# Memory and first weights in one transfer per row tile, and a closing layer norm without GpSimd

## The chip, the cores and the metric

The kernel runs on one core of a Trainium2 chip. The metric is the device time of one execution in microseconds (us), as the median over several runs. A trace of one profiled execution shows what each engine did: TensorE (PE, with its weight loads as PEld), VectorE (DVE), ScalarE (ACT), GpSimd (POOL) and SyncE (SP), which here only issues transfers.

## The reference

One layer of a hybrid decoder trunk for 256 tokens of width 2,048, in fp32. One input projection feeds eight causal attention heads with rotary positions, a gated MLP and four heads of cross attention into 256 memory tokens; a last projection, the residual and a layer norm close it.

```python
proj = x @ w_in                                   # 2048 x 6656, cut into nine parts
y_mo = moba_attention(rope(q_mo), rope(k_mo), v_mo) * silu(g_mo)   # one block of 256: causal attention
y_gm = gmlp_spatial_gate(u_gm, v_gm, ...) * silu(g_gm)
mem_k, mem_v = split(mem @ w_mem_kv)              # 256 memory tokens
y_me = memory_attention(q_me, mem_k, mem_v) * silu(g_me)
sub = concatenate([y_mo, y_gm, y_me]) @ w_out
x = layer_norm(2 ** 0.25 * x + sub, ln_g, ln_b)   # over the 2048 columns of a token
```

## The kernel before

The precision of fp32 is reached with two parts: an operand is split into a high part in the type float32r and a low part that holds the rest, and a product is made of three matmuls, high by high, high by low and low by high (`mm3`, lines 103 to 107). `split` (lines 99 to 101) makes the high part on ScalarE and then the low part on VectorE.

All weights come in one stream (`STREAM`, lines 39 to 52), in items in the order of use. An item is cut into pieces of 1,024 elements per partition (512 KB). An item marked "T" has 128 columns of weights as the stationary operand and yields the projection transposed (`proj_t`); an item marked "N" has up to 512 columns as the moving operand and yields two PSUM tiles of 128 tokens each (`proj_n`). The 2,048 rows of a contraction are 16 row tiles of 128. `load_piece` (from line 128) takes one of six raw buffers, issues the transfer on SP and splits it into one of four pairs of high and low buffers; `next_pieces` calls it three pieces ahead of use (`LEAD`). Nothing but these buffers, and the order in which the instructions stand on each engine, sets when things happen; a scheduler turns the waits into semaphores.

The first item is the memory's values: `mem` by 512 columns of `w_mem_kv`, 16 row tiles, two PSUM tiles. Both operands must come from memory for it. Its first piece holds two row tiles, and lines 136 to 145 treat them apart. For row tile 0 the memory (128 KB) and the weights (twice 128 KB) come in three transfers and go into exact fp32 matmuls without a split (lines 226 to 231). Row tile 1 comes as 128 KB of memory and 256 KB of weights. From piece 1 on, a transfer of 512 KB of weights and one of 256 KB of memory (`load_act`, line 158) bring two row tiles at a time. Before all that, seven matmuls on zeros (line 114) keep TensorE at work while the first transfers are under way. The items behind it load `x` in the same way, two row tiles at a time.

At the end, the output projection runs over 2,048 columns in items of 512, 512, 512, 256 and 256 (`OUT_COLS`). VectorE adds the residual to each PSUM tile (line 562) and takes the statistics (line 564). In the last item the two token tiles are made one after the other (`apart`), and `finish(t)` (from line 527) closes a token tile: mean and variance, an inverse root on GpSimd (line 334), then five column blocks (`FINISH`). The first block of 512 columns is normed by ScalarE (line 540) and gets gain and bias from GpSimd (lines 541 and 542); the other four (512, 512, 256, 256) are done by VectorE in two steps each, one that subtracts the mean and multiplies by the gain (line 544) and one that multiplies by the inverse root and adds the bias (line 545). SP stores the four blocks of VectorE, the ACT queue that of GpSimd.

## Time and profile before

| | |
|---|---|
| Median of 3 runs | 468.15 us (467.88 to 468.91) |
| Span of the profiled execution | 466.4 us (first to last instruction); its own run time is not given apart from the runs |
| Busy share of the span | PE 96%, PEld 83%, DVE 74%, ACT 50%, POOL 3% |
| Chain that ended last | PE 94%, DVE 3%, DMA 1% |
| Moved by DMA | 91.79 MB, mean 197 GB/s |

The span and all moments are counted from the first instruction. Busy shares are averages over the whole span. In a row of a timeline the first number is the start and the second the duration; what stands in brackets is how long the engine had been idle and what ended it. A duration is longer than the time from one instruction's start to the next one's where an engine overlaps them. The granted clock of TensorE is 1.00 where it runs at its full 2.4 GHz.

### The profile page before, as it was taken

To read this page: it belongs to the slowest core of one execution; us is meant where nothing else is said; L and a number is where in the kernel's file an instruction comes from. 1 tells how busy PE (TensorE), PEld (TensorE's weight loads), DVE (VectorE), ACT (ScalarE), POOL (GpSimd) and SP (SyncE) were. 2 spreads that over 40 slices of the span, in tenths; PEclk is the share of its full clock that TensorE was granted. 3 is DMA by queue.
4 is the path that set the end of the run, shared out by engine and by line. 5 is a ranking of instruction groups with operands and counts; after the bars stand their busy time and mean duration, and the time that the engine had idled before them with its cause. 6 is when DMAs were issued, how large, how long until landed. Compare 5 with 4: busy or idle time off the path is not lost.

```text
span 466.4 us, 6674 instructions
## 1 busy us (share of the span) xinstructions
PE 449.5 (96%) x2465; PEld 386.9 (83%) x2465; DVE 343.5 (74%) x582; ACT 231.3 (50%) x357; POOL 14.4 (3%) x23
## 2 busy tenths in 40 slices
PE   6999999999999999999999999999999999999980
PEld 3888888888888888888888888888888888888980
DVE  3879866776677988885778888858988746465666
ACT  4765754665444555554445545545655543334300
POOL 1000000000000000000000000000200000000033
PEclk9999999999999999999999999999999999999996
DMA  7998776545465555545655455876565557575123
GB/s 268 322 348 275 286 272 225 172 149 161 155 196 179 176 169 182 180 160 163 210 187 180 151 176 200 295 220 204 171 214 181 181 184 237 207 227 184 27 65 135
DMA packets 29552, 91.79 MB, mean 197 GB/s; under 512 B 3408, under 2 KB 5072, under 8 KB 29520
## 3 DMA queue, kind: packets, MB, share of 16 engines
q1 hardware_dynamic: 29232, 90.85, 58.9%
q10 hardware_dynamic: 288, 0.52, 0.3%
q8 instruction: 19, 0.31, 0.3%
q14 instruction: 13, 0.11, 0.1%
HBM read 89.26 MB, written 2.10 MB: 196 GB/s over the span
## 4 chain that ended last, share of the span: by engine, by line
PE 94%; DVE 3%; DMA 1%; SPq 0%; issue 0%; ACT 0%; DVEq 0%
PE acc L195 35%; PE acc L196 18%; PE acc L105 12%; PE acc L106 12%; PE acc L107 12%; DVE hX L544 2%; DMA wraw<-weights 1%; PE ptp L390 1%; DVE hX L545 1%; PE sc L105 1%; PE sc L106 0%; PE sc L107 0%; PE pv L107 0%; PE pv L105 0%; PE pv L106 0%
## 5 line engine op out<-in xcount | busy, mean ns | idle before, releaser
L101 DVE TENSOR_TENSOR wlo<-wraw,whi 128x1024 fp32r<-128x1024 f32 (+1 forms) x152 | 185.5, 1220 | 92.0 <-ACT whi L100 90.7
L100 ACT ACTIVATE whi<-wraw 128x1024 fp32r<-128x1024 f32 (+1 forms) x152 | 160.5, 1056 | 167.6 <-PE acc L195 61.8
L195 PE MATMUL acc<-xX,whi 128*128 128x512 f32 x640 | 227.4, 399 | 0.0
L196 PE MATMUL acc<-xX,wlo 128*128 128x256 f32 x640 | 179.4, 280 | 0.0
L195 PEld LDWEIGHTS acc<-xX,whi 128*128 128x128 f32 x640 | 120.2, 188 | 28.0
L196 PEld LDWEIGHTS acc<-xX,wlo 128*128 128x128 f32 x640 | 120.8, 189 | 0.1
L105 PE MATMUL acc<-whi,yX 128*128 128x512 f32 (+1 forms) x160 | 55.5, 347 | 0.0
L107 PE MATMUL acc<-whi,yX 128*128 128x512 f32 (+1 forms) x160 | 55.5, 347 | 0.0
L106 PE MATMUL acc<-wlo,yX 128*128 128x512 f32 (+1 forms) x160 | 55.5, 347 | 0.0
L105 PE MATMUL acc<-whi,xX 128*128 128x512 f32 x96 | 38.1, 397 | 0.0
L107 PE MATMUL acc<-whi,xX 128*128 128x512 f32 x96 | 37.5, 391 | 0.0
L106 PE MATMUL acc<-wlo,xX 128*128 128x512 f32 x96 | 37.4, 390 | 0.0
L105 PEld LDWEIGHTS acc<-whi,yX 128*128 128x128 f32 x160 | 30.3, 189 | 3.8
L107 PEld LDWEIGHTS acc<-whi,yX 128*128 128x128 f32 x160 | 30.3, 189 | 3.8
L106 PEld LDWEIGHTS acc<-wlo,yX 128*128 128x128 f32 x160 | 30.3, 189 | 3.7
L195 PE MATMUL acc<-memX,whi 128*128 128x512 f32 x64 | 22.6, 399 | 0.0
L107 PEld LDWEIGHTS acc<-whi,xX 128*128 128x128 f32 x96 | 18.0, 188 | 4.0
L105 PEld LDWEIGHTS acc<-whi,xX 128*128 128x128 f32 x96 | 18.0, 188 | 3.4
L106 PEld LDWEIGHTS acc<-wlo,xX 128*128 128x128 f32 x96 | 18.0, 188 | 3.3
L202 DVE TENSOR_TENSOR projT<-acc,part 128x256 f32<-128x256 f32 x44 | 18.1, 413 | 0.0
L196 PE MATMUL acc<-memX,wlo 128*128 128x256 f32 x64 | 18.0, 281 | 0.0
L200 ACT ACTIVATE part<-acc 128x256 f32<-128x256 f32 x44 | 16.1, 369 | 0.0
(147 smaller groups left out, 411.0 us busy)
## 6 DMA issues: line engine op xcount, KB each, us to landing
wraw<-weights SPq DMA_DIRECT2D x151, 512.0 KB, 3.5
araw<-xT SPq DMA_DIRECT2D x8, 256.0 KB, 4.5
araw<-memT SPq DMA_DIRECT2D x7, 256.0 KB, 5.8
xs<-xrow SPq DMA_DIRECT2D x6, 256.0 KB, 4.4
lnp<-ln_gv SPq DMA_DIRECT2D x4, 256.0 KB, 4.5
lnp<-ln_bv SPq DMA_DIRECT2D x4, 256.0 KB, 5.3
out<-hX SPq DMA_DIRECT2D x4, 256.0 KB, 2.6
xs<-xrow SPq DMA_DIRECT2D x4, 128.0 KB, 3.3
```

What stands on the lines that cost most here:

```text
L100: nc.scalar.activation(hi, src, AF.Copy)
L101: nc.vector.tensor_tensor(out=lo, in0=src, in1=f32(hi), op=ALU.subtract)
L105: nc.tensor.matmul(o, a[0], b[0], start=start, stop=False)
L106: nc.tensor.matmul(o, a[0], b[1], start=False, stop=False)
L107: nc.tensor.matmul(o, a[1], b[0], start=False, stop=stop)
L195: nc.tensor.matmul(flat, hi[:, m, :], X[:, k].rearrange("p a s -> p (a s)"), start=k == 0, stop=False)
L196: nc.tensor.matmul(acc[:, 0, :], lo[:, m, :], X[:, k, 0, :], start=False, stop=k == KT - 1)
L200: nc.scalar.activation(part, acc[:, 1, :], AF.Copy)
L202: nc.vector.tensor_tensor(out=r, in0=acc[:, 0, :], in1=part, op=ALU.add)
L390: nc.tensor.transpose(tp[:, n, :], st["p"][:, at[t] // P + b, :], ident)
L544: nc.vector.scalar_tensor_tensor(out=o, in0=o, scalar=mvr[:, 0:1], in1=g, op0=ALU.subtract, op1=ALU.mult)
L545: nc.vector.scalar_tensor_tensor(out=o, in0=o, scalar=rs, in1=b, op0=ALU.mult, op1=ALU.add)
```

## The change

The first item becomes an item of its own kind, "H". The host lays each row tile of the memory (256 columns) beside the 512 columns of weights of the same rows, 768 elements per partition, 384 KB without a gap, and one transfer brings both (line 142 of the new kernel). There are 16 such pieces of one row tile each, where 8 pieces of two row tiles and as many transfers of memory were before. All 16 row tiles are split and take six matmuls each; the four exact matmuls of row tile 0 go. In row tile 0 VectorE makes the memory's high part, in the others ScalarE. The pieces use the same six raw buffers and the four pairs of split buffers. In this item the matmuls of both PSUM tiles alternate, first high by high, then memory low by weights high, then memory high by weights low. `mm3` takes the same order everywhere.

In `finish` VectorE does all five blocks in its two steps. Two subtract steps (`AHEAD`) stand ahead of the first step that needs the inverse root. ScalarE's pass, GpSimd's two passes and the product of mean and inverse root go. The stores go in turn through the ACT queue (blocks 0, 2 and 4) and the SP queue (blocks 1 and 3).

```diff
+STREAM = [("H", "mem", 4 * P, NW)] + [("T", "mem", b) for b in range(4)]
-STREAM = [("N", "mem", 4 * P, NW)] + [("T", "mem", b) for b in range(4)]
...
+AHEAD = 2
...
 def pieces_of(item):
+    if item[0] == "H":
+        return KT, 1, item[3]
...
     def mm3(o, a, b, start, stop):
         nc.tensor.matmul(o, a[0], b[0], start=start, stop=False)
-        nc.tensor.matmul(o, a[0], b[1], start=False, stop=False)
-        nc.tensor.matmul(o, a[1], b[0], start=False, stop=stop)
+        nc.tensor.matmul(o, a[1], b[0], start=False, stop=False)
+        nc.tensor.matmul(o, a[0], b[1], start=False, stop=stop)
...
     def load_piece(n):
...
-        if n == 0:
-            a = wp.tile([P, S], F32, tag="araw", name="araw0", bufs=3)
-            nc.sync.dma_start(a, memT[:, 0, :])
-            for c in range(0, width, S):
-                nc.sync.dma_start(raw[:, 0, c:c + S], src[:, 0, c:c + S])
-            first.update(a=a, w=raw[:, 0, :])
-            load_act(memT, memX, 1, 1)
-            nc.sync.dma_start(raw[:, 1, :], src[:, 1, :])
-            split(hi[:, 1, :], lo[:, 1, :], raw[:, 1, :])
+        if STREAM[i][0] == "H":
+            both = wp.tile([P, PIECE], F32, tag="wraw", name="hraw", bufs=6)[:, :S + width]
+            nc.sync.dma_start(both, head[j])
+            if j == 0:
+                nc.vector.tensor_copy(memX[:, j, 0, :], both[:, :S])
+            else:
+                nc.scalar.activation(memX[:, j, 0, :], both[:, :S], AF.Copy)
+            nc.vector.tensor_tensor(out=memX[:, j, 1, :], in0=both[:, :S], in1=f32(memX[:, j, 0, :]), op=ALU.subtract)
+            split(hi[:, 0, :], lo[:, 0, :], both[:, S:])
         else:
-            nc.sync.dma_start(raw, src)
+            raw = wp.tile([P, kts, width], F32, tag="wraw", name="wraw", bufs=6)
+            nc.sync.dma_start(raw, w[n - KT].rearrange("p (k n) -> p k n", k=kts))
             split(hi, lo, raw)
-        if n == 1:
-            split(memX[:, 0, 0, :], memX[:, 0, 1, :], first["a"])
-        if 0 < n < first_piece[1]:
-            load_act(memT, memX, kts * n, kts)
...
     def proj_n(X, order=range(KT), hook=None, apart=False):
...
-                if X is memX and k == 0:
-                    for c in range(0, width, S):
-                        for t in range(NT):
-                            nc.tensor.matmul(acc[t][:, c:c + S], first["a"][:, t * P:(t + 1) * P],
-                                             first["w"][:, c:c + S], start=c == 0, stop=False)
-                    continue
+                if X is memX:
+                    for a, b in ((0, hi), (1, hi), (0, lo)):
+                        for t in range(NT):
+                            nc.tensor.matmul(acc[t], X[:, k, a, tk[t]], b[:, m, :], start=k == 0 and a == 0 and b is hi,
+                                             stop=k == KT - 1 and b is lo)
...
     def finish(t):
...
-        nm = work.tile([P, 1], F32, tag="nm", name="nm")
-        neg = work.tile([P, 1], F32, tag="neg", name="neg")
-        nc.vector.tensor_scalar(out=neg, in0=mvr[:, 0:1], scalar1=-1.0, scalar2=None, op0=ALU.mult)
-        nc.gpsimd.tensor_tensor(out=nm, in0=neg, in1=rs, op=ALU.mult)
-        for c, wd in FINISH:
-            cs, ls = slice(c, c + wd), slice(c % NW, c % NW + wd)
-            o, g, b = hX[:, t, cs], lg[c // NW][:, ls], lb[c // NW][:, ls]
-            if c == 0:
-                nc.scalar.activation(o, o, AF.Identity, scale=rs, bias=nm)
-                nc.gpsimd.tensor_tensor(out=o, in0=o, in1=g, op=ALU.mult)
-                nc.gpsimd.tensor_tensor(out=o, in0=o, in1=b, op=ALU.add)
-            else:
-                nc.vector.scalar_tensor_tensor(out=o, in0=o, scalar=mvr[:, 0:1], in1=g, op0=ALU.subtract, op1=ALU.mult)
-                nc.vector.scalar_tensor_tensor(out=o, in0=o, scalar=rs, in1=b, op0=ALU.mult, op1=ALU.add)
-            if c:
-                nc.sync.dma_start(out[t, :, cs], o)
-        cs = slice(0, FINISH[0][1])
-        nc.scalar.dma_start(out[t, :, cs], hX[:, t, cs])
+        def centre(c, wd):
+            o, g, _ = part(c, wd)
+            nc.vector.scalar_tensor_tensor(out=o, in0=o, scalar=mvr[:, 0:1], in1=g, op0=ALU.subtract, op1=ALU.mult)
+
+        for c, wd in FINISH[:AHEAD]:
+            centre(c, wd)
+        for n, (c, wd) in enumerate(FINISH):
+            if n >= AHEAD:
+                centre(c, wd)
+            o, _, b = part(c, wd)
+            nc.vector.scalar_tensor_tensor(out=o, in0=o, scalar=rs, in1=b, op0=ALU.mult, op1=ALU.add)
+            (nc.sync if n % 2 else nc.scalar).dma_start(out[t, :, c:c + wd], o)
...
+    memT, c = stationary(mem), STREAM[0][2]
+    head = np.concatenate([memT.transpose(1, 0, 2), mats["mem"][:, c:c + NW].reshape(KT, P, NW)], axis=2)
```

The order of the transfers on SP at the start, before:

```order
L138 DMA araw_108<-memT 128x256
L140 DMA wraw<-weights 128x256 x2
L160 DMA araw<-memT 128x256
L143 DMA wraw<-weights 128x512
L146 DMA wraw<-weights 128x1024
L160 DMA araw<-memT 128x512
L146 DMA wraw<-weights 128x1024
L160 DMA araw<-memT 128x512
L146 DMA wraw<-weights 128x1024
```

and now:

```order
L142 DMA hraw<-head 128x768 x16
L151 DMA wraw<-weights 128x1024 x4
L161 DMA araw<-xT 128x512
L261 DMA posi<-pos 128x256
L263 DMA invf<-inv_freq 128x1
L151 DMA wraw<-weights 128x1024
L161 DMA araw<-xT 128x512
```

Ten issues of 128 to 512 KB, for the first six row tiles and the weights of two more, have become one issue per row tile (`hraw` is a raw buffer with both operands, `head` the tensor in memory).

TensorE's first matmuls on data, before (`araw_108` is the memory's row tile 0):

```order
L229 MATMUL acc<-wraw,araw_108 128x256 x4
L105 MATMUL acc<-whi,memX 128x512 x2
L106 MATMUL acc<-wlo,memX 128x512
L107 MATMUL acc<-whi,memX 128x512
L106 MATMUL acc<-wlo,memX 128x512
L107 MATMUL acc<-whi,memX 128x512
L105 MATMUL acc<-whi,memX 128x512 x2
L106 MATMUL acc<-wlo,memX 128x512 x2
```

and now, from row tile 0 on:

```order
L231 MATMUL acc<-whi,memX 128x512 x4
L231 MATMUL acc<-wlo,memX 128x512 x2
L231 MATMUL acc<-whi,memX 128x512 x4
L231 MATMUL acc<-wlo,memX 128x512 x2
L231 MATMUL acc<-whi,memX 128x512 x4
L231 MATMUL acc<-wlo,memX 128x512 x2
```

The unsplit fp32 product is gone, and every row tile reads four times with the high weights before it needs the low ones.

VectorE from the inverse root's input of the first token tile to the second tile's residual step (`omv` mean and variance, `ors` the inverse root, `lnp` gain or bias), before:

```order
L333 TENSOR_SCALAR rsq<-omv 128x1
L534 TENSOR_SCALAR neg<-omv 128x1
L544 SCALAR_TENSOR_TENSOR hX<-hX,omv,lnp 128x512 x2
L545 SCALAR_TENSOR_TENSOR hX<-hX,ors,lnp 128x512 x2
L544 SCALAR_TENSOR_TENSOR hX<-hX,omv,lnp 128x256 x2
L545 SCALAR_TENSOR_TENSOR hX<-hX,ors,lnp 128x256 x2
L562 SCALAR_TENSOR_TENSOR hX<-xs,acc 128x256
L564 BN_STATS obn_3790<-hX 128x6
```

and now:

```order
L334 TENSOR_SCALAR rsq<-omv 128x1
L539 SCALAR_TENSOR_TENSOR hX<-hX,omv,lnp 128x512 x2
L547 SCALAR_TENSOR_TENSOR hX<-hX,ors,lnp 128x512 x2
L539 SCALAR_TENSOR_TENSOR hX<-hX,omv,lnp 128x512
L539 SCALAR_TENSOR_TENSOR hX<-hX,omv,lnp 128x256
L547 SCALAR_TENSOR_TENSOR hX<-hX,ors,lnp 128x512
L547 SCALAR_TENSOR_TENSOR hX<-hX,ors,lnp 128x256
L539 SCALAR_TENSOR_TENSOR hX<-hX,omv,lnp 128x256
L561 SCALAR_TENSOR_TENSOR hX<-xs,acc 128x256
L547 SCALAR_TENSOR_TENSOR hX<-hX,ors,lnp 128x256
L563 BN_STATS obn_3834<-hX 128x6
```

Two steps of 512 columns have come in, the negation has gone, and the residual step of the second tile stands ahead of the last scale step of the first.

## Rows read from the trace of the kernel before

**Rows 1.** Page: the head

```profile
span 466.4 us, 6674 instructions
```

**Rows 2.** Busy time by stretch: PE, PEld, DVE, ACT, POOL; clock, DMA share, GB/s

```profile
4.00:12.20 8.20, 5.71 (x21) 3.35 (x21) 3.04 (x5) 3.81 (x6) 0.00 (x0) 1.00 0.93 347
12.20:453.00 440.80, 440.80 (x2439) 382.35 (x2438) 329.98 (x558) 224.98 (x349) 7.55 (x10) 1.00 0.60 197
```

**Rows 3.** PE waits, 0 to 12.5 us: us in total, times, longest

```profile
PE acc L105 <- ACT whi L100: 1.5, 1, 1.5
PE acc L105 <- ACT memX L100: 1.0, 1, 1.0
```

**Rows 4.** ACT timeline, first stage: start us, us; what ended its wait

```profile
3.04 0.42 ACT L100 ACTIVATE memX<-araw 128x256 fp32r<-128x256 f32 x1 [0.96 <-DMA araw<-memT]
4.95 0.42 ACT L100 ACTIVATE memX<-araw 128x256 fp32r<-128x256 f32 x1 [1.49 <-DMA araw<-memT]
6.89 0.63 ACT L100 ACTIVATE whi<-wraw 128x512 fp32r<-128x512 f32 x1 [1.53 <-DMA wraw<-weights]
8.86 1.06 ACT L100 ACTIVATE whi<-wraw 128x1024 fp32r<-128x1024 f32 x1 [1.33 <-DMA wraw<-weights]
24.24 0.63 ACT L100 ACTIVATE memX<-araw 128x512 fp32r<-128x512 f32 x1 [1.51 <-DMA araw<-memT]
```

**Rows 5.** PE timeline, either end of the unbroken first item

```profile
12.40 0.40 PE L105 MATMUL acc<-whi,memX 128*128 128x512 f32 x1
30.09 0.39 PE L195 MATMUL acc<-memX,whi 128*128 128x512 f32 x1
```

**Rows 6.** DVE timeline of the first closing norm

```profile
448.88 0.14 DVE L534 TENSOR_SCALAR neg<-omv 128x1 f32<-128x1 f32 x1
448.94 0.74 DVE L544 SCALAR_TENSOR_TENSOR hX<-hX,omv,lnp 128x512 f32<-128x512 f32 x1
451.59 1.51 DVE L544 SCALAR_TENSOR_TENSOR hX<-hX,omv,lnp 128x256 f32<-128x256 f32 x1
453.03 1.48 DVE L544 SCALAR_TENSOR_TENSOR hX<-hX,omv,lnp 128x256 f32<-128x256 f32 x1
454.44 0.87 DVE L545 SCALAR_TENSOR_TENSOR hX<-hX,ors,lnp 128x256 f32<-128x256 f32 x2
```

**Rows 7.** POOL timeline beside it

```profile
449.12 0.98 POOL L334 TENSOR_TENSOR ors<-rsq 128x1 f32<-128x1 f32 x1 [119.38 <-DVE neg L534]
451.32 1.50 POOL L541 TENSOR_TENSOR hX<-hX,lnp 128x512 f32<-128x512 f32 x1 [0.93 <-ACT hX L540]
452.90 1.33 POOL L542 TENSOR_TENSOR hX<-hX,lnp 128x512 f32<-128x512 f32 x1
```

**Rows 8.** SP timeline: the last store

```profile
462.97 0.41 SPq L547 DMA_DIRECT2D out<-hX  x1
```

**Rows 9.** SP timeline at the start (moments of issue)

```profile
0.80 0.39 SPq L138 DMA_DIRECT2D araw<-memT  x1
2.66 0.43 SPq L143 DMA_DIRECT2D wraw<-weights  x1
```

**Rows 10.** Tile wraw, 250 to 330 us: issue to landing of 512 KB

```profile
DMA to landing us min/median/max: 3.1/3.4/5.1
```

**Rows 11.** ACT by form, 0 to 36 us: count, busy us, mean ns, idle

```profile
L100 ACT ACTIVATE memX<-araw 128x256 fp32r<-128x256 f32 x2 | 0.8, 416 | 2.4 <-DMA araw<-memT 2.4
L100 ACT ACTIVATE whi<-wraw 128x512 fp32r<-128x512 f32 x1 | 0.6, 629 | 1.5 <-DMA wraw<-weights 1.5
```

**Rows 12.** DVE by form, 0 to 36 us, same columns

```profile
L101 DVE TENSOR_TENSOR memX<-araw,memX 128x256 fp32r<-128x256 f32 x2 | 0.8, 425 | 3.8 <-ACT memX L100 3.8
L101 DVE TENSOR_TENSOR wlo<-wraw,whi 128x512 fp32r<-128x512 f32 x1 | 0.7, 693 | 1.7 <-ACT whi L100 1.7
```

**Rows 13.** DVE timeline, low parts of the next three weight pieces

```profile
26.72 3.78 DVE L101 TENSOR_TENSOR wlo<-wraw,whi 128x1024 fp32r<-128x1024 f32 x3 [1.12 <-ACT whi L100]
```

**Rows 14.** DMA issues, 448 to 467 us: count, KB each, us to landing

```profile
out<-hX ACTq DMA_DIRECT2D x2, 256.0 KB, 2.6
```

More of the change, by code (lines that the diff above doesn't have):

```diff
@@ L76, in hymba_layer @@
 @with_exitstack
-def hymba_layer(ctx: ExitStack, tc: tile.TileContext, xT, memT, x, pos, inv_freq, w, wsT, b_s,
+def hymba_layer(ctx: ExitStack, tc: tile.TileContext, xT, head, x, pos, inv_freq, w, wsT, b_s,
                 gln_g, gln_b, ln_g, ln_b, out):
@@ L125, in hymba_layer @@
             first_piece[i] = n
-    ready, first = {}, {}
+    ready = {}
     def load_piece(n):
@@ L205, in proj_n @@
     def proj_n(X, order=range(KT), hook=None, apart=False):
-        assert STREAM[item[0]][0] == "N"
+        assert STREAM[item[0]][0] in "HN"
         width = STREAM[item[0]][3]
@@ L225, in proj_n @@
                 k = order[j * kts + m]
-                if X is memX and k == 0:
-                    for c in range(0, width, S):
+                tk = [slice(t * P, (t + 1) * P) for t in range(NT)]
+                if X is memX:
+                    for a, b in ((0, hi), (1, hi), (0, lo)):
                         for t in range(NT):
-                            nc.tensor.matmul(acc[t][:, c:c + S], first["a"][:, t * P:(t + 1) * P],
-                                             first["w"][:, c:c + S], start=c == 0, stop=False)
-                    continue
-                for t in range(NT):
-                    tk = slice(t * P, (t + 1) * P)
-                    mm3(acc[t], (X[:, k, 0, tk], X[:, k, 1, tk]), (hi[:, m, :], lo[:, m, :]),
-                        j + m == 0, j * kts + m == KT - 1)
+                            nc.tensor.matmul(acc[t], X[:, k, a, tk[t]], b[:, m, :], start=k == 0 and a == 0 and b is hi,
+                                             stop=k == KT - 1 and b is lo)
+                else:
+                    for t in range(NT):
+                        mm3(acc[t], (X[:, k, 0, tk[t]], X[:, k, 1, tk[t]]), (hi[:, m, :], lo[:, m, :]),
+                            j + m == 0, j * kts + m == KT - 1)
                 pump()
@@ L531, in finish, with part @@
         rsqrt(rs, mvr[:, 1:2], LN_EPS)
[L532 to L549 removed]
+        def part(c, wd):
+            return hX[:, t, c:c + wd], lg[c // NW][:, c % NW:c % NW + wd], lb[c // NW][:, c % NW:c % NW + wd]
+        def centre(c, wd):
[9 more added lines that the diff above has]
+            (nc.sync if n % 2 else nc.scalar).dma_start(out[t, :, c:c + wd], o)
     for n, (c, wd) in enumerate(OUT_COLS):
@@ L578 @@
     stream = []
-    for item in STREAM:
+    memT, c = stationary(mem), STREAM[0][2]
+    head = np.concatenate([memT.transpose(1, 0, 2), mats["mem"][:, c:c + NW].reshape(KT, P, NW)], axis=2)
+    for item in STREAM[1:]:
         n, kts, width = pieces_of(item)
@@ L585 @@
         "xT": stationary(x),
-        "memT": stationary(mem),
+        "head": head,
         "xrow": x[0].reshape(NT, P, D),
```

2 lines of the change are left out of this document (removed).

## Prediction

> **What bounds the kernel now.** I read the page's head, then the busy time by stretch, the waits of TensorE, the timelines of the first stage, and last the timelines of VectorE, GpSimd and the stores at the end. The profiled span is 466.4 us [rows 1]. The runs give no separate time for the profiled execution; their median, 468.15 us, is 1.75 us above the span, and I carry these 1.75 us over.
>
> The reader should see three parts. From 12.20 to 453.00 us TensorE is busy for 440.80 of 440.80 us, with the granted clock at 1.00 [rows 2]: nothing ends a wait there, and only fewer matmuls could shorten it. Before that, from 4.00 to 12.20 us, it is busy for 5.71 of 8.20 us [rows 2]. Both of its waits for data lie there: 1.5 us for the high part of the first weights and 1.0 us for that of the memory, both made by ScalarE [rows 3]. ScalarE in turn waits for transfers [rows 4]. In that stage ScalarE starts as each transfer lands, so its starts give the arrivals: 128 KB by 3.04 us, 512 KB by 4.95, 768 KB by 6.89, 1,280 KB by 8.86, and all 6,144 KB of the first item (memory and weights) by 24.24 us [rows 4]. The third part is the time after the last matmul, some 13 us, where VectorE works off two closing norms and the last store goes out at 462.97 us [rows 8].
>
> The first item's last matmul is followed by the next item at 30.09 us [rows 5]. Between 12.40 and 30.09 us lie 13 row tiles of 6 matmuls, so one takes 17.69/78 = 0.227 us and a row tile 1.36 us. The question at the start is how much earlier than 30.09 us the next item begins; since TensorE never pauses after that, all of it reaches the end.
>
> **The start.** The change removes the four exact fp32 matmuls of row tile 0 and gives it six split ones like the others: 96 matmuls, 96 x 0.227 = 21.8 us. If they ran without a pause from moment t, the next item would begin at t + 21.8.
>
> *When can they start?* One transfer of 384 KB is issued at the same 0.80 us [rows 9]. 128 KB landed 2.24 us after that issue [rows 4, 9], and 512 KB take at least 3.1 us [rows 10]; 384 KB two thirds of the way between are 2.8 us, landing at 3.6. ScalarE then makes the high weights in 0.63 us [rows 11] and TensorE starts some 0.05 us later, at 4.3. The seven warming matmuls, unchanged, stand ahead of it; I allow 0.1 us for them. VectorE makes the memory's high and low parts in under 0.9 us, and the low weights in 0.69 us [rows 12], which the order high-high, low-high, high-low covers: the first four matmuls take 0.9 us. So t = 4.4 and the best case is 4.4 + 21.8 = 26.2 us, a gain of 3.9.
>
> *Does piece 1 come in time?* Its ScalarE work is 0.42 + 0.63 us [rows 11], so it can be used 1.1 us after landing, and 15 row tiles (20.4 us) follow. In the kernel before, 768 KB had landed at 6.89 us [rows 4], with the last of them issued at 2.66 us [rows 9]. Now two issues make up these 768 KB; at the old pitch of four issues in 1.86 us [rows 9] the second goes at 1.27, 1.4 us sooner. I take the landing 1.4 us sooner too, at 5.5 us: use at 6.6, next item at 6.6 + 20.4 = 27.0 us. The worst case keeps the old arrivals by bytes: piece 1 at 6.89, piece 2 (1,152 KB, between the last two arrivals) at 8.4; 8.4 + 1.1 + 14 x 1.36 = 28.5 us. The gain thus lies between 1.6 and 3.9 us; I take **3.0**, from the shifted arrival, whose row is nearest in bytes.
>
> *Later pieces.* From 8.86 to 24.24 us 4,864 KB came [rows 4], 1.21 us for 384 KB, less than the 1.36 us in which TensorE uses them. Per piece ScalarE has 1.05 us of work and VectorE 1.12 [rows 11, 12]; both fit. The six raw buffers let six transfers queue, so SP waits on VectorE's last read of a buffer only from piece 6 on. Even unchanged arrivals would do for the last piece: 24.24 + 1.1 + 1.36 = 26.7 us. Of the next item's weights, the first low part was ready at 26.72 + 1.26 = 28.0 us before [rows 13]; were it no earlier, TensorE would pause under 0.8 us there. I count nothing, as no transfer of the stage gets later and the pieces behind it have 2 us and more in hand.
>
> Here a rule speaks against the change. The row says that 256 and 512 KB transfers, queued behind one another, came at 4,864 KB in 15.4 us [rows 4], so their fixed time overlaps. The Trainium skill, page "DMA: Bandwidth & Descriptors", section "Bandwidth", would have transfers batched to at least 1 MiB, and this change cuts some from 512 to 384 KB. By the row the term stays 3.0; by that rule it would shrink or turn, which is the third rival.
>
> **The order of the three products** (high-low last, everywhere) moves no time: TensorE waits for nothing after 12.20 us [rows 2], and the number of loads and matmuls per row tile is the same.
>
> **The end.** VectorE's two passes over 512 columns cost 2.65 us for four steps from 448.94 to 451.59, 0.66 each; the two 256-column subtract steps take 1.44 and 1.41 us from start to start, though half as wide, and the two 256-column scale steps 0.87 together [rows 6]. The slow ones stand exactly beside GpSimd's two passes over 512 columns: these end at 452.82 and 454.23, VectorE's at 453.10 and 454.51, each 0.28 us later [rows 6, 7]. I read this as VectorE held until GpSimd is done. The change takes those passes and ScalarE's away and gives VectorE two more 512-column steps. Per row block: before 2.65 + 2.85 + 0.87 = 6.37; now 6 x 0.66 + 4 x 0.435 = 5.7. That saves 0.66, and the dropped negation 0.06 [rows 6]. Both blocks lie end to end on VectorE (the second accumulator is complete soon after 453.00 us [rows 2], VectorE is free only at 454.44 + 0.87 = 455.31 [rows 6]), so twice 0.72 = 1.44. The last scale step now follows directly on its own input, and starts when that ends: under 0.1 us back. **1.4**.
>
> Is the inverse root late? GpSimd gives it at 449.12 + 0.98 = 450.10 us [rows 7]; two subtract steps from 448.88 end their turn at 450.20. The margin is 0.1 us, so at worst some tenths come back: 1.2 at the low end, 1.5 at the high. The store queues: SP's old issues wait on VectorE, not on each other; ACT's stores land in 2.6 us [rows 14], and each waits only for VectorE. ScalarE has nothing else to do then. Splitting the stores over two queues counts nothing, and the last store moves with VectorE's end.
>
> **Sum.** 466.4 - 3.0 - 1.4 = 462.0 us of span, + 1.75 = **463.7 us**.
>
> **The rivals.** *Early transfers stay as slow as now* (0.15): the arrivals by bytes do not move, the start gains 1.6 and the end 1.2 to 1.4, 465.2 us. For it: from 4.95 to 6.89 us only 256 KB landed, with five transfers already issued. Against: the old stage began with four transfers of 128 KB, issue by issue.
>
> *The narrow subtract step is slow of itself* (0.04): then each block costs 3.96 + 2.85 + 0.87 = 7.7 us, 1.3 more than now, less the negation; the end loses 2.5, and 466.4 - 3.0 + 2.5 + 1.75 = 467.6, no change that can be told. Against it: 512 columns take half that time.
>
> *The smaller pieces come more slowly than TensorE uses them* (0.03), the side on which it is slower. The slowest stretch of the trace brought 768 KB from 4.95 to 8.86 us [rows 4], 1.95 us for 384 KB. At that pace the last piece lands at 3.6 + 15 x 1.95 = 32.9, the next item starts 2.5 us later at 35.4 against 30.09, and with the end's 1.4 the kernel takes 468.15 + 5.3 - 1.4 = 472 us. It turns slower from 1.7 us per piece on: (30.09 + 1.4 - 2.5 - 3.6)/15. This is where the skill's rule on batching would bite; the rows after 8.86 us speak against it.
>
> *The start gains but the next item waits for its weights* (0.05): up to 0.8 us back, 464.5.
>
> **How the numbers follow.** The forecast has the remaining 0.73; with its bounds (start 2.2 to 3.9, end 1.2 to 1.5) it reaches from 462.7 to 464.8. Adding the first and the last rival, and a little for run to run, the range is 462.4 to 465.6. A measurement tells about 0.2%, 0.94 us, from no change. Faster: 0.73 + 0.15 + 0.05 = 0.93; same: 0.04; slower: 0.03.
>
> **What would show it.** Right: the second item's first matmul near 27 us, TensorE's only wait between row tiles 0 and 1, at most about 1 us; no pause after that; subtract steps of 256 columns near 0.45 us; the last store 4 to 5 us earlier. Wrong: TensorE waiting for ScalarE at every row tile (pace), a 256-column step still near 1.4 us (not GpSimd), or VectorE idle before the first scale step (inverse root late).

## The result, and the profile after

The changed kernel takes 463.77 us (median of four runs, 463.63 to 464.22); the kernel before, on the same chip, 468.15 us (467.88 to 468.91). The ratio is 0.9897, 95% interval 0.9878 to 0.9917. The profiled execution took 463.88 us with a span of 462.2 us, 1.68 us more than the span.

Busy time by stretch answers to [rows 2]; columns as there, the last stretch ends with the last store's issue:

```profile
4.00:12.20 8.20, 7.55 (x29) 5.28 (x29) 6.37 (x14) 5.89 (x13) 0.00 (x0) 1.00 0.97 348
12.20:448.00 435.80, 435.80 (x2407) 377.80 (x2406) 326.10 (x563) 223.83 (x356) 4.13 (x7) 1.00 0.57 198
448.00:459.00 11.00, 2.84 (x24) 2.63 (x22) 10.83 (x22) 0.00 (x0) 0.93 (x1) 0.83 0.46 160
```

TensorE is now busy for 7.55 of the first 8.20 us instead of 5.71, and still without a gap in the long middle. Its waits for data in the first 30 us (us in total, times, longest) answer to [rows 3]:

```profile
PE acc L231 <- ACT whi L106: 0.6, 2, 0.3
```

So 2.5 us of waiting became 0.6, but still in two places. ScalarE's timeline gives the arrivals, as in [rows 4]: the first start, and each start after a wait for a transfer, is a row tile that has landed.

```profile
3.80 0.63 ACT L106 ACTIVATE whi<-hraw 128x512 fp32r<-128x512 f32 x1 [1.73 <-DMA hraw<-head]
5.47 0.42 ACT L146 ACTIVATE memX<-hraw 128x256 fp32r<-128x256 f32 x1 [1.04 <-DMA hraw<-head]
...
7.47 0.42 ACT L146 ACTIVATE memX<-hraw 128x256 fp32r<-128x256 f32 x1 [1.06 <-DMA hraw<-head]
...
8.55 0.42 ACT L146 ACTIVATE memX<-hraw 128x256 fp32r<-128x256 f32 x1
```

Row tiles 0, 1 and 2 are there at 3.80, 5.47 and 7.47 us; from row tile 3 on ScalarE finds each one waiting. TensorE's timeline shows what that costs:

```profile
4.49 1.27 PE L231 MATMUL acc<-whi,memX 128*128 128x512 f32 x4
...
6.46 1.19 PE L231 MATMUL acc<-whi,memX 128*128 128x512 f32 x4 [0.24 <-ACT whi L106]
...
8.46 1.20 PE L231 MATMUL acc<-whi,memX 128*128 128x512 f32 x4 [0.34 <-ACT whi L106]
...
9.95 1.07 PE L231 MATMUL acc<-whi,memX 128*128 128x512 f32 x4
...
27.63 0.39 PE L196 MATMUL acc<-memX,whi 128*128 128x512 f32 x1
```

From start to start, waits included, row tiles 0 and 1 take 1.97 and 2.00 us each, row tile 2 1.49, all others 1.36. The next item starts at 27.63 us instead of 30.09 [rows 5]: 2.46 us. In the kernel before, TensorE came to row tile 2 here:

```profile
10.48 0.73 PE L105 MATMUL acc<-whi,memX 128*128 128x512 f32 x2 [0.98 <-ACT memX L100]
```

So it is there 10.48 - 8.46 = 2.02 us sooner: 1.39 us because the row tile lands at 7.47 us instead of 8.86 [rows 4], and 0.63 us because ScalarE's work takes 0.99 us from there to TensorE's start instead of 1.62, as a transfer brings one row tile and not two. Nearly all of the other 0.44 us lie in row tile 2 itself, which took 1.92 us before (to 12.40 [rows 5]) and now takes 1.49.

The end, VectorE's timeline of the second closing norm (the first one's steps have the same durations), beside [rows 6]:

```profile
445.12 0.42 DVE L561 SCALAR_TENSOR_TENSOR hX<-xs,acc 128x256 f32<-128x256 f32 x1 [3.55 <-PE acc L113]
...
453.17 1.40 DVE L539 SCALAR_TENSOR_TENSOR hX<-hX,omv,lnp 128x512 f32<-128x512 f32 x2
454.50 1.41 DVE L547 SCALAR_TENSOR_TENSOR hX<-hX,ors,lnp 128x512 f32<-128x512 f32 x2
455.82 1.14 DVE L539 SCALAR_TENSOR_TENSOR hX<-hX,omv,lnp 128x512 f32<-128x512 f32 x2
456.88 1.14 DVE L547 SCALAR_TENSOR_TENSOR hX<-hX,ors,lnp 128x512 f32<-128x512 f32 x2
457.94 0.48 DVE L539 SCALAR_TENSOR_TENSOR hX<-hX,omv,lnp 128x256 f32<-128x256 f32 x1
458.45 0.48 DVE L547 SCALAR_TENSOR_TENSOR hX<-hX,ors,lnp 128x256 f32<-128x256 f32 x1
```

(A pair of 1.14 us is one step of 512 columns and one of 256; the view gives the first one's form.) The 256-column subtract step takes 0.48 us instead of 1.48 to 1.51, and nothing waits for the inverse root, which is GpSimd's only work left [rows 7]:

```profile
446.67 0.92 POOL L335 TENSOR_TENSOR ors<-rsq 128x1 f32<-128x1 f32 x1 [119.33 <-DVE rsq L334]
453.40 0.93 POOL L335 TENSOR_TENSOR ors<-rsq 128x1 f32<-128x1 f32 x1 [5.81 <-DVE rsq L334]
```

In the kernel before, the first closing residual stood here:

```profile
447.57 0.42 DVE L562 SCALAR_TENSOR_TENSOR hX<-xs,acc 128x256 f32<-128x256 f32 x1 [3.44 <-PE acc L107]
```

The last store, ScalarE's queue (the issue) and the issues from 458.5 us on (count, KB, us to landing), beside [rows 8, 14]:

```profile
458.97 0.34 ACTq L548 DMA_DIRECT2D out<-hX  x1
```

```profile
out<-hX ACTq DMA_DIRECT2D x1, 128.0 KB, 2.1
```

From the first closing residual of the last columns to the last store's issue it was 462.97 - 447.57 = 15.40 us; it is 458.97 - 445.12 = 13.85, 1.55 us less. From there to the span's end 3.43 us became 3.23. So 2.46 + 1.55 + 0.20 = 4.2 us, which is the whole difference of the spans; from the second item's first matmul to the first closing residual both kernels take 417.48 us to within 0.01.

### The profile page after: what moved, and what is told of

The parts are those of the page before. It is cut to its first block, busy times and chain, and to the rows that moved or that the text cites. A ratio compares the mean times of both kernels' runs of the same rounds, so it can differ in the third digit from the quotient of the medians.

```text
span 462.2 us, 6713 instructions
## 1 busy us (share of the span) xinstructions
PE 448.9 (97%) x2463; PEld 386.6 (84%) x2463; DVE 343.8 (74%) x600; ACT 231.2 (50%) x369; POOL 6.6 (1%) x17
## 4 chain that ended last, share of the span: by engine, by line
PE 94%; DVE 3%; DMA 1%; issue 0%; ACT 0%; SPq 0%
PE acc L196 36%; PE acc L197 18%; PE acc L111 11%; PE acc L113 11%; PE acc L112 11%; PE acc L231 4%; DMA hraw<-head 1%; DVE hX L547 1%; PE ptp L391 1%; DVE hX L539 1%; PE sc L111 1%; PE sc L112 0%; PE sc L113 0%; PE pv L113 0%; PE pv L111 0%
## 5 line engine op out<-in xcount | busy, mean ns | idle before, releaser
L107 DVE TENSOR_TENSOR wlo<-wraw,whi 128x1024 fp32r<-128x1024 f32 x144 | 176.1, 1224 | 86.9 <-ACT whi L106 84.8
L106 ACT ACTIVATE whi<-wraw 128x1024 fp32r<-128x1024 f32 x144 | 152.3, 1059 | 159.2 <-PE acc L196 58.0
L231 PE MATMUL acc<-whi,memX 128*128 128x512 f32 x64 | 17.6, 396 | 0.6 <-ACT whi L106 0.6
```

The source lines that it names most:

```text
L106: nc.scalar.activation(hi, src, AF.Copy)
L107: nc.vector.tensor_tensor(out=lo, in0=src, in1=f32(hi), op=ALU.subtract)
L231: nc.tensor.matmul(acc[t], X[:, k, a, tk[t]], b[:, m, :], start=k == 0 and a == 0 and b is hi, stop=k == KT - 1 and b is lo)
```

## Experiments

Each was run beside the kernel before on the same chip; ratios are to that kernel.

### The start alone, the end alone

The closing norm of the kernel before, put into the changed kernel, and the reverse:

```diff
 # e1: finish(t) is that of the kernel before; all else as in the changed kernel
 # e2: the kernel before, with finish(t) of the changed kernel and
+AHEAD = 2
```

> The change's start and its order of the three products, with the closing norm of the kernel before (ScalarE and GpSimd take the first block, negation included). Theory: start and end add up and do not touch each other; the second item begins at about 27.6 us as after the change, the last store goes out some 15.4 us after the first closing residual step as before, total 468.15 - 2.5 = 465.7 us (465.3 to 466.0). Rival: what the start gains is worth less or more once the end is the old one (the store tail or the weights at the end hold it); then the total is under 465 or over 466.5 us.

> The kernel before with the change's closing norm alone. Theory: GpSimd's passes held VectorE; without them the closing work from the first residual step to the last store takes 13.85 us instead of 15.4, total 468.15 - 1.6 = 466.5 us (466.2 to 466.9); 256-column subtract steps at 0.48 us. Rival: the narrow subtract step is slow of itself; then they stay near 1.4 us and the total is 470 us or more.

The start alone: 465.55 us (465.03 to 466.0), ratio 0.9927 [0.9901, 0.9953]; its second item starts at 28.01 us, and its 256-column subtract steps are slow as before, 2.92 and 2.88 us for two. The end alone: 467.69 us (465.84 to 468.24), ratio 0.9967 [0.9947, 0.9987]; 256-column steps of 0.48 us, and again 13.85 us from the first closing residual to the last store's issue. By the ratios, 0.73% and 0.33% come to 1.06%, beside the whole change's 1.03%, but each of them is known to 0.2 or 0.3% only, and six of the twelve runs of the kernel before that they are measured against lie in the upper group that the last experiment is about. The traces are firmer. From the second item to the first closing residual it is 417.48 us in both, as before and as after the change; from there to the last store's issue it is 15.4 us with the old end and 13.85 with the new. The two parts add up and do not touch each other. That the end alone came 1.2 us above the expectation has another cause, which follows below.

### What sets the start

Four edits, each undoing or moving one thing: the old order of the products in `mm3`, that is everywhere but in the first item, which keeps its own new order; row tile 0 unsplit; memory and weights of a row tile in two transfers on the same queue; and ScalarE's copy of the memory put on VectorE.

```diff
 # e3, mm3
-        nc.tensor.matmul(o, a[1], b[0], start=False, stop=False)
-        nc.tensor.matmul(o, a[0], b[1], start=False, stop=stop)
+        nc.tensor.matmul(o, a[0], b[1], start=False, stop=False)
+        nc.tensor.matmul(o, a[1], b[0], start=False, stop=stop)
 # e9, load_piece
-            nc.sync.dma_start(both, head[j])
+            nc.sync.dma_start(both[:, :S], head[j][:, :S])
+            nc.sync.dma_start(both[:, S:], head[j][:, S:])
 # e4, load_piece; VectorE keeps the order copy, memory low, weights low
-            if j == 0:
+            if j < 3:
                 nc.vector.tensor_copy(memX[:, j, 0, :], both[:, :S])
 # e8, proj_n: row tile 0 is multiplied as it is, memory is split beside row tile 3
+                if X is memX and k == 0:
+                    for c in range(0, width, S):
+                        for t in range(NT):
+                            nc.tensor.matmul(acc[t][:, c:c + S], first["a"][:, t * P:(t + 1) * P],
+                                             first["w"][:, c:c + S], start=c == 0, stop=False)
```

> The changed kernel with the old order of the three products outside the first item (high-high, high-low, low-high). Theory: TensorE waits for no operand after the first stage, so the order is worth nothing: 463.8 us, within 0.3. Rival: the low weights come late somewhere in the output projection or the attention and the new order hides it; then TensorE shows waits after 12 us and the total rises by 0.5 us or more.

> The changed kernel with each piece of the first item brought by two transfers, 128 KB of memory and 256 KB of weights, instead of one of 384 KB; everything else as changed. Theory: what one transfer per row tile buys at the start is issue time; two issues of some 0.46 us per piece put the second piece's last issue at 2.2 us instead of 1.25, and its arrival 0.5 to 1 us later than 5.5 us: second item at 28.1 to 28.6 us, total 464.3 to 464.8 us. Rival: the arrivals are set by the transfer engines alone, not by the issues; then the second piece still lands at 5.5 us and the total stays at 463.8 us.

> The changed kernel, with the high part of memory's row tiles 1 and 2 made on VectorE and no longer on ScalarE, so that ScalarE makes only the weights' high part there (0.6 us after a transfer lands, and no copy of memory ahead of it). In the changed kernel TensorE waits 0.24 us before row tile 1 and 0.34 us before row tile 2 for ScalarE's copies. My theory (part of the lost start is the two copies in series on ScalarE behind each arrival): the weights' high part of row tiles 1 and 2 is ready about 0.25 us earlier, the second item starts at 27.2 to 27.5 us instead of 27.63, and the time falls by 0.2 to 0.4 us to 463.3 to 463.6 us. Rival (TensorE waits for the transfers alone, and VectorE's copy, its low part behind it, makes the weights' low part later by as much): second item at 27.6 to 27.8, time 463.7 to 464.0 us.

> The changed kernel with row tile 0 as an unsplit fp32 product again (eight matmuls of 256 columns, 1.89 us in the profile of before, in place of six of 512 columns behind the copy), loaded by the new single transfer; memory's two parts of row tile 0 are made later, beside row tile 3. My theory (TensorE waits for row tiles 1 and 2 in any case, so a row tile 0 that starts 0.6 us earlier and takes 0.5 us longer moves nothing): second item at 27.4 to 27.9 us, time 463.5 to 464.2 us, the same as the changed kernel. Rival (splitting row tile 0 was part of the gain): second item at 28.1 us or later, time 464.3 to 465.0 us.

Measured: e3 463.87 us, ratio 0.9893 [0.9871, 0.9915]; e9 463.97, 0.9904 [0.9876, 0.9933]; e4 463.51, 0.9896 [0.9880, 0.9913]; e8 463.78, 0.9896 [0.9877, 0.9915]. None can be told from the changed kernel. For e9 that is a miss of mine in the time, but not in the arrivals:

```profile
4.41 0.63 ACT L106 ACTIVATE whi<-hraw 128x512 fp32r<-128x512 f32 x1 [2.33 <-DMA hraw<-head]
...
6.56 0.63 ACT L106 ACTIVATE whi<-hraw 128x512 fp32r<-128x512 f32 x1 [1.21 <-DMA hraw<-head]
```

```profile
7.24 1.21 PE L232 MATMUL acc<-whi,memX 128*128 128x512 f32 x4 [0.48 <-ACT whi L106]
```

With two issues for each row tile, row tiles 0 and 1 are complete 0.6 and 1.1 us later than in the changed kernel (3.80 and 5.47 us), as I had expected. But the memory of row tile 1 lands ahead of its weights and is copied by then, TensorE can use the row tile 0.68 us after it has landed, and it does not wait for row tile 2: its last wait is the one before row tile 1, and the second item starts at 27.81 us, 0.18 us later than in the changed kernel. So bringing both operands in one transfer makes the first row tiles earlier and still buys no time that the runs can tell.

In the others the last wait is for row tile 2. Where it lands, and where the second item starts, in us from the span's start:

| kernel | row tile 2 landed | second item | between |
|---|---|---|---|
| changed | 7.47 | 27.63 | 20.16 |
| e1, old end | 7.85 | 28.01 | 20.16 |
| e3, old product order | 7.49 | 27.65 | 20.16 |
| e6, one store queue (below) | 7.57 | 27.73 | 20.16 |
| e8, row tile 0 unsplit | 7.33 | 27.50 | 20.17 |
| e4, memory's copy on VectorE | 7.64 | 27.50 | 19.86 |

Whatever is done to row tiles 0 and 1 here, the item starts a fixed time after row tile 2's landing: ScalarE's two copies and 14 row tiles. Only e4 changes that, by 0.30 us, since there the memory's copy is off ScalarE; it lands in the time as 0.1 to 0.3 us, less than the runs tell apart (e6, run beside it with the changed kernel's start, took 463.54 us). Splitting row tile 0 is worth nothing by itself. So of what the change does to the start, neither the split nor the single transfer explains the 2.46 us when taken alone. What is left is the size of a piece, one row tile instead of two, and the order of the products within the first item; no run changes one of these alone, so it stays an argument that the size does it.

### Why row tile 2 lands late

Between 4 and 6 us the transfer engines move 200 and 264 GB/s, half to two thirds of what they do later. That is not all. For each transfer the trace keeps 16 marks of completion, as many as the core has transfer engines, and the transfer has landed with the last of them. In the changed kernel row tile 0's marks lie between 3.35 and 3.78 us. Of row tile 1's, fifteen are there by 4.76 us and the last comes at 5.45. Of row tile 2's, eight are there by 6.12 us and fifteen by 6.66, and the last comes at 7.45, when nine of row tile 3's are there already. The other five kernels of the table show the same: half of row tile 2 by 5.69 to 6.15 us, the last mark at 7.31 to 7.83. So what TensorE waits for is the last parts of row tile 2, while parts of later row tiles are already complete. Three edits bring in the second queue; all three also keep SyncE's other loads in their place, and e13 the first steps of VectorE and ScalarE.

```diff
 # e7: six raw buffers are filled at once, in turn by two queues
+                (nc.scalar if e in (1, 3, 5) else nc.sync).dma_start(early[e], head[e])
 # e10: each of the six in two halves of 64 partitions
+                    nc.sync.dma_start(early[e][:P // 2], head[e][:P // 2])
+                    nc.scalar.dma_start(early[e][P // 2:], head[e][P // 2:])
 # e13: e4, and ScalarE issues row tiles 2 and 4 behind a tiny activation
+                nc.scalar.activation(tiny[:, 1:2], tiny[:, 0:1], AF.Copy)
+                (nc.scalar if e in (2, 4) else nc.sync).dma_start(early[e], head[e])
```

> The changed kernel with the first six row tiles' transfers issued in turn by SyncE and ScalarE, at once at the start. My theory (row tiles 1 and 2 come late because the 16 transfer engines move too little between 3.9 and 6.6 us, 170 to 300 GB/s, whichever queue issued them): arrivals as in the changed kernel, 5.2 to 5.7 us for piece 1 and 7.2 to 7.7 for piece 2, second item at 27.4 to 27.9 us, time 463.5 to 464.2 us. Rival (one queue's issue or its order of service sets the arrivals): pieces 1 and 2 land 0.5 to 1 us earlier, second item at 26.6 to 27.2 us, time 462.7 to 463.3 us. It can also go the other way: pieces that run side by side share the engines and land together, piece 1 at 6.5 us or later, and the second item at 28.3 us or later, time above 464.4 us.

> The changed kernel with each of the first six row tiles' transfers cut into two halves of 64 partitions, one issued by SyncE and one by ScalarE. With whole row tiles in turn on two queues the slow stretch of 170 to 300 GB/s between 3.9 and 6.6 us was gone (400 to 415 GB/s from 3 us on), but row tile 0 shared the engines and landed 1.2 us later. My theory now (one queue alone doesn't keep the transfer engines full there): two queues move the halves in order, row tile 0 lands at 3.6 to 4.1 us, row tiles 1 and 2 at 4.6 to 5.2 and 5.6 to 6.2; TensorE starts on data at 4.5 to 5.0 us and hardly waits, the second item starts at 26.4 to 27.1 us, the span is 460.9 to 461.6 us. The time above the span was 2.05 us instead of 1.7 in the two-queue run, so I expect 462.6 to 463.4 us. Rival (the slow stretch lies in the transfer engines or the memory and only moved, to the stretch before 2.8 us): row tile 0 lands at 4.3 us or later, second item at 27.3 to 27.8, time 463.8 to 464.2 us.

> The changed kernel with memory's high part of row tiles 0 to 2 on VectorE, and with row tiles 2 and 4 issued by ScalarE, behind a tiny activation that draws its table load (1.28 us) ahead of the two issues; SyncE issues the others. So row tile 0 has the transfer engines to itself, and the second queue comes in at about 3.6 us. My theory (one queue alone leaves the engines short between 3.9 and 6.6 us, two keep them at 400 GB/s and more): row tile 0 lands at 3.6 to 3.9 us and row tiles 1 and 2 together at 5.3 to 5.7, TensorE waits 0.3 to 0.5 us once, before row tile 1, and the second item starts at 26.5 to 26.9 us instead of 27.63; time 462.5 to 463.0 us, or up to 0.3 us more if the time above the span grows as it did with whole row tiles on two queues. Rival (the slow stretch is not the queue's, but comes to whatever moves at that time): row tiles 1 and 2 land at 6.0 us or later, second item at 27.4 us or later, time 463.4 us or more.

Stretches of the changed kernel, then of e7 (the last columns: granted clock, DMA share, GB/s):

```profile
4.00:5.00 1.00, 0.93 (x3) 0.47 (x3) 0.97 (x3) 0.43 (x1) 0.00 (x0) 1.00 0.70 200
5.00:6.00 1.00, 1.00 (x6) 0.65 (x4) 0.24 (x2) 0.53 (x2) 0.00 (x0) 1.00 0.95 264
6.00:7.00 1.00, 0.76 (x3) 0.49 (x3) 0.90 (x2) 0.41 (x1) 0.00 (x0) 1.00 0.92 341
...
8.00:9.00 1.00, 0.66 (x3) 0.49 (x3) 0.91 (x2) 0.85 (x3) 0.00 (x0) 1.00 1.02 412
9.00:10.00 1.00, 1.00 (x6) 0.79 (x5) 0.94 (x3) 0.99 (x3) 0.00 (x0) 1.00 1.04 418
```

```profile
4.00:5.00 1.00, 0.29 (x1) 0.00 (x0) 0.16 (x1) 0.16 (x1) 0.00 (x0) 1.00 1.04 412
5.00:6.00 1.00, 0.47 (x2) 0.43 (x3) 0.97 (x3) 1.00 (x3) 0.00 (x0) 1.00 1.01 399
6.00:7.00 1.00, 1.00 (x6) 0.81 (x5) 1.00 (x3) 0.62 (x2) 0.00 (x0) 1.00 1.04 415
```

*e7* took 464.02 us, ratio 0.9917 [0.9901, 0.9934]. My theory had the time right and the mechanism wrong: the slow stretch is gone, row tile 2's 16 marks come within 0.8 us (5.86 to 6.66) and it lands at 6.68 us, but row tile 0, which shares the engines with row tile 1, only at 4.84, so TensorE waits 1.2 us at the very start and the second item begins at 27.42. The span is 461.9 us, 0.3 less than the changed kernel's, yet the time above the span is 2.02 to 2.08 us in all four runs, where it is 1.67 to 1.79 in every other kernel here. What adds these 0.3 us stays open.

*e10* took 469.31 us, ratio 1.0018 [1.0005, 1.0031]; neither theory's number holds. ScalarE's timeline, its queue's issues first:

```profile
0.80 6.09 ACTq L145 DMA_DIRECT2D hraw<-head  x6
6.92 1.28 ACT L106 ACT_TABLE_LOAD   x1 [6.92 <-DMA hraw<-head]
8.22 0.63 ACT L106 ACTIVATE whi<-hraw 128x512 fp32r<-128x512 f32 x1
```

ScalarE was at its six issues until 6.9 us (four were out by 3.6 us, the fifth not before 4.9) and came to its table load and the first high weights 4.4 us late, while VectorE had been able to use row tile 0 from 4.88 us. TensorE waited 4.5 us in one piece. And the halves moved at 237 to 317 GB/s between 3 and 10 us with the engines fully busy. So a second queue does not bring the rate by itself; and the time of this run says that an engine that computes pays for its queue's issues.

*e13* took 463.60 us, ratio 0.9897 [0.9881, 0.9914]. The engines moved 366 to 412 GB/s from 3 to 9 us. Row tile 1 was there at 6.16 us and row tile 2 by 6.7, 0.8 us earlier than in the changed kernel; the only wait for data is 0.27 us ahead of row tile 0. But ScalarE's two issues had gone out at 1.26 us, beside its table load and not behind it, so row tile 1 shared the engines and came 0.7 us later; and the first matmuls were slow, which is told in the last section. Second item at 27.75 us; this trace is of the slowest of the four runs (464.13 us, the others 463.55 to 463.63). The time fits the rival, the rates between 3 and 9 us my theory. In e7 and e13 the slow stretch is gone with the second queue, in e10 it is not, and a stretch of 246 GB/s came in e13 from 9 to 10 us. What makes it is not settled. None of these versions beats the changed kernel by more than the runs tell apart.

### What held VectorE's narrow steps

Two useless passes on GpSimd for each token tile, as wide as those that the change removed:

```diff
+        scr = work.tile([P, NW], F32, tag="gl", name="scr")
+        nc.gpsimd.tensor_tensor(out=scr, in0=lg[0], in1=rs.to_broadcast([P, NW]), op=ALU.mult)
+        nc.gpsimd.tensor_tensor(out=scr, in0=scr, in1=lb[0], op=ALU.add)
```

> The changed kernel with two useless GpSimd passes of 512 columns added for each token tile, right behind the inverse root, on a scratch tile that nothing reads; VectorE's work and the stores stay. My theory (it was GpSimd's two-input passes that held VectorE's 256-column subtract steps at 1.44 us in the kernel before): VectorE's closing steps that fall into the last token tile's passes are held again, by 0.8 to 1.0 us for each of one to three steps; the block from the first closing residual to the last store's issue grows from 13.85 us to 15 to 17 us, and the time to 465 to 467 us. Rival (the narrow subtract was slow by its place, behind a residual of fresh data or a PSUM read, and not by GpSimd): every 256-column step stays at 0.48 us, every 512-column one at 0.74, and the time at 463.6 to 464.0 us.

467.23 us (466.67 to 467.84), ratio 0.9971 [0.9959, 0.9982]: 3.7 us more than e6, which ran beside it. VectorE and GpSimd in the second closing norm:

```profile
455.96 1.07 POOL L535 TENSOR_TENSOR scr<-lnp,ors 128x512 f32<-128x512 f32 x1
457.10 1.59 POOL L536 TENSOR_TENSOR scr<-scr,lnp 128x512 f32<-128x512 f32 x1
```

```profile
456.05 3.19 DVE L551 SCALAR_TENSOR_TENSOR hX<-hX,ors,lnp 128x512 f32<-128x512 f32 x2
...
457.50 1.74 DVE L551 SCALAR_TENSOR_TENSOR hX<-hX,ors,lnp 128x512 f32<-128x512 f32 x1
...
461.28 0.47 DVE L543 SCALAR_TENSOR_TENSOR hX<-hX,omv,lnp 128x256 f32<-128x256 f32 x1
```

Now it is the 512-column scale steps that stand beside GpSimd, and they are the slow ones: 3.19 us for two instead of 1.41, in both norms, so 2 x 1.8 = 3.6 us, which is the difference but for 0.1. (From the first closing residual to the last step's start it is 16.94 us, 13.33 in the changed kernel.) The 256-column steps, with GpSimd done, take 0.47. It is not a step's kind or width; it is who runs beside it. My expectation of 465 to 467 us had counted only one to three held steps of the last tile; four are held, since both norms lie end to end on VectorE. The Trainium skill, page "SBUF — State Buffer", section "SBUF: two separate sides", says that a VectorE step with two SBUF inputs and a GpSimd step that reads SBUF exclude each other for a whole instruction. The trace agrees: the second step ends at 459.24 us, 0.55 after GpSimd's second pass.

### The store queues

```diff
-            (nc.sync if n % 2 else nc.scalar).dma_start(out[t, :, c:c + wd], o)
+            nc.sync.dma_start(out[t, :, c:c + wd], o)
```

> The changed kernel with all closing stores issued by SyncE, as in the kernel before, instead of by SyncE and ScalarE in turn. My theory, as in the prediction (the two queues are worth nothing, since the last store is issued when VectorE's last step is done and finds its queue empty): last store issued within 0.1 us of where it is in the changed kernel, landing 2.1 to 2.6 us, time 463.5 to 464.2 us, which is the same within 0.2%. Rival (one queue's issues, about 0.65 us apart like VectorE's steps, pile up on SyncE): last store issued 0.3 to 0.8 us later, time 464.2 to 464.8 us.

463.54 us (463.25 to 463.95), ratio 0.9900 [0.9885, 0.9915]; span 462.2 us. The two queues are worth nothing here, as predicted.

### Two groups of runs in the kernel before

The kernel before has runs around 468 and others some 1.5 us above; the end alone, which has the old start, has both too (four at 465.84 to 466.36, six at 467.58 to 468.24), and its profile is of the upper group. Twelve runs of a kernel with its waits filled test where they come from:

```diff
+                    for _ in range(4):
+                        nc.tensor.matmul(idle, zero[:, :P], zero, start=True, stop=True)
                     continue
...
+                if X is memX and k == 1 and STREAM[item[0] - 1][0] == "N":
+                    for _ in range(4):
+                        nc.tensor.matmul(idle, zero[:, :P], zero, start=True, stop=True)
```

> The kernel before, with four more matmuls on zeros (0.85 us of TensorE's time) behind row tile 0 and four behind row tile 1 of the first item, where TensorE waits 1.5 and 1.0 us in the profiled execution of before. The kernel before has two groups of runs, 468.0 to 468.5 and 469.4 to 469.9 us, and in the profile of the kernel with the old start and the new end TensorE waited 2.3 us there and then ran at a granted clock of 0.50 for 3.4 us. My theory (the upper group are runs in which such a wait was long enough that the clock fell): with the waits partly filled the clock stays at 1.00 in the start, the upper group is gone, and all runs lie within 0.8 us of one another, at 467.9 to 468.7 us. Rival (the two groups have another cause, such as the transfers' own times): two groups 1.2 to 1.8 us apart remain, with a quarter to a third of the runs in the upper one.

468.40 us (467.64 to 468.81), ratio 0.9996 [0.9983, 1.0008]. No run lies in the upper group; of the 23 runs of before beside it seven do (469.40 to 470.06), with a mean granted clock of 0.986 or 0.987, where the other sixteen have 0.989 to 0.991. Stretches of the end alone, then of this kernel (the column ahead of the last two is the granted clock):

```profile
10.00:12.00 2.00, 1.31 (x5) 1.08 (x6) 1.04 (x2) 1.35 (x2) 0.00 (x0) 0.89 1.03 411
12.00:15.00 3.00, 3.00 (x9) 2.33 (x8) 2.51 (x3) 2.44 (x4) 0.00 (x0) 0.51 0.98 362
15.00:20.00 5.00, 5.00 (x24) 4.12 (x23) 4.75 (x6) 3.35 (x5) 0.00 (x0) 1.00 0.96 313
```

```profile
10.00:12.00 2.00, 1.76 (x7) 0.77 (x6) 1.72 (x3) 1.47 (x3) 0.00 (x0) 1.00 1.04 417
12.00:15.00 3.00, 3.00 (x14) 2.45 (x14) 2.86 (x3) 2.20 (x4) 0.00 (x0) 1.00 0.87 339
```

In the end alone TensorE had waited 2.3 us, from 8.39 to 10.69, and then did 9 matmuls in 3 us instead of 14, at a granted clock of 0.51, its lower level of 1.2 GHz; with the waits filled (0.2 us left) no fall is on record. The end alone starts its second item at 31.48 us, 1.39 us later than in the profile of the kernel before. So the upper group is the price of a long wait in the old start; for the kernel before itself this rests on its runs' granted clocks and on the filled waits, as its one trace is not of that group. The runs spread over 1.2 us, more than the 0.8 I expected, but without a gap. The changed kernel's own waits are 0.34 us at most, and its runs lie within 0.6 us; one run each of e7 and e9, which wait longer, lies 1.6 us above its others, but with the same granted clock (0.992), so what slowed these two is not shown.

## Why the prediction was right, by its own steps

**The sum.** Forecast: a span of 462.0 and a time of 463.7 us; measured 462.2 and 463.77. The likeliest case held. That the time is met to 0.1 us is luck: the start gave 0.54 us less than forecast, the end 0.35 us more, and the two nearly cancel.

**The start: 3.0 forecast, 2.46 measured.** The first matmul on data came at 4.49 us (4.4 forecast), row tile 0 landed at 3.80 (3.6), row tile 1 at 5.47 (5.5), usable at 6.46 (6.6). The 5.5 came from the earlier issue, and e9 bears that reasoning out: there the last issue for row tile 1 is at 2.17 us instead of 1.24 and the landing at 6.56 instead of 5.47. The close agreement is in part luck all the same, since in the table's other kernels, with the same issues, row tile 1 landed at 4.8 to 5.2 us. The step that was mis-sized is "Does piece 1 come in time?": it let row tile 2 and all behind it come at least as fast as TensorE uses them. Counting back from 27.0 us, row tile 2 had to land by 27.0 - 20.16 = 6.84 us; it landed at 7.47, 2.00 us behind row tile 1, though fifteen of its sixteen marks were there by 6.66. That is the second wait, which the forecast "TensorE's only wait between row tiles 0 and 1" excluded, and the 0.63 us by which 27.63 missed 27.0. The rival *early transfers stay as slow as now* had this half right: it priced row tile 2 at 8.4 us.

**Later pieces.** No pause from row tile 3 on, and none at the second item: right, and the rivals on pace and on the next item's weights fall. The Trainium skill, page "DMA: Bandwidth & Descriptors", section "Bandwidth", has transfers batched to at least 1 MiB, next to figures for transfers that GpSimd issues; by that rule transfers of 384 KB should have lost to larger ones. The trace does not agree here: issued by SyncE and queued behind one another they move at 412 and 418 GB/s from 8 to 10 us.

**The order of the products** moved no time outside the first item (e3), nor did the **two store queues** (e6): right. No run brings the old order back in the first item.

**The end: 1.4 forecast, 1.55 measured, and 0.20 from the last store's landing.** The reason, VectorE held by GpSimd, is shown by e5 from both sides, and the rival of a slow narrow step falls. The subtract steps take 0.48 us; the inverse root is never waited for. The stretch from the last store's issue to the span's end was taken as unchanged; it fell from 3.43 to 3.23 us, and with one store queue (e6) it is as short, 459.06 to 462.2.

**The 1.75 us above the span** were 1.68 in the profiled run.

## What to carry to other kernels

Where a first stage waits for transfers, find the last row tile that is waited for and count from its landing; work on the ones ahead of it moves nothing, as five kernels with the same 20.16 us show, until one of those becomes the last that is waited for, as in e9. A transfer counts as landed with the last of its sixteen parts, so a mean rate does not tell when it is there. Count every engine beside VectorE's closing steps as part of them: two GpSimd passes that look free cost 1.8 us for each norm. A second queue for loads costs its engine the issues, and shares the transfer engines with the transfer that is wanted first.

## What the runs showed of the hardware

- A wait of 2.3 us early in the program was followed by some 3 us at the lower clock. With such waits filled, the two groups of runs of one kernel became one.
- A granted clock of 1.00 in a row is no measurement ahead of the trace's first clock mark. That mark stands at 4.67 us in the changed kernel, at 7.20 in e13 and at 12.41 in e10; before it the rows read 1.00 in any case. In these three, matmuls of 512 columns stand 0.43 us apart up to about the mark, as those at 0.51 did, and 0.23 us behind it: TensorE ran at its lower level, 1.2 GHz, until then. In e13 this fell on row tile 0, which took 2.63 us instead of 1.36:

```profile
5.29 1.05 PE L238 MATMUL acc<-whi,memX 128*128 128x512 f32 x2
...
6.14 0.63 PE L238 MATMUL acc<-whi,memX 128*128 128x512 f32 x1
...
6.57 0.92 PE L238 MATMUL acc<-wlo,memX 128*128 128x512 f32 x2
...
7.33 1.09 PE L238 MATMUL acc<-whi,memX 128*128 128x512 f32 x4
```

```profile
5.00:6.00 1.00, 1.00 (x3) 0.81 (x3) 0.37 (x1) 0.00 (x0) 0.00 (x0) 1.00 0.98 366
```

  In e10 it fell on the matmuls behind the wait of 4.5 us, from 8.90 to 12.46 us. In e7, whose mark stands at 4.03 us, the first five behind a wait of 1.2 us stand 0.26 us apart. What decides when the clock rises is open.
- A mark can mislead too. In e5 the clock reads 0.95 over the whole middle, yet from the second item to the first closing residual it takes 417.33 us, and 417.49 in the changed kernel at 1.00:

```profile
12.20:448.00 435.80, 435.80 (x2409) 378.13 (x2408) 326.84 (x563) 224.16 (x355) 4.75 (x8) 0.95 0.58 198
```

- Six transfers issued by ScalarE held its own work until 6.9 us, three only until 2.2 us.
- One arrangement of queues (e7) added 0.3 us outside the span, in every run.
